# An encoder layer on one core: the product of memory values and output weight leaves the first stage and becomes filler work, per head, in the chain and mLSTM stages

## The chip, the cores and the metric

The kernel runs on one core of a Trainium2 chip. The metric is device time in microseconds. In a profile PE is TensorE (PEld its weight loads), DVE is VectorE, ACT is ScalarE, POOL is GpSimd and SP is SyncE, which issues nearly all DMAs; L115 is line 115 of the kernel.

## The reference, cut to what matters

One layer with a mixer (an input projection of the normalised x, four head groups that end in one output projection) and a cross-attention of 4 heads into 256 memory tokens. The change concerns the values of the cross-attention:

```
def memory_cross_attention(h, mem_n, wq, wkv, wo):
    q = split_heads(h @ wq, N_MEM_HEADS)
    k, v = jnp.split(mem_n @ wkv, 2, axis=-1)
    k, v = split_heads(k, N_MEM_HEADS), split_heads(v, N_MEM_HEADS)
    logits = jnp.einsum("bhtd,bhmd->bhtm", q, k).astype(jnp.float32) * (MEM_HEAD_DIM ** -0.5)
    p = jax.nn.softmax(logits, axis=-1)
    o = jnp.einsum("bhtm,bhmd->bhtd", p.astype(v.dtype), v)
    return merge_heads(o) @ wo
```

The memory is 256 x 1024, wkv 1024 x 2048, wo 1024 x 1024, x 1024 x 1024. Both kernels use that (p v) wo = p (v wo): for each head they form v wo, a matrix of 256 x 1024 from 256 x 256 and 256 x 1024, store it in DRAM as vwd, and multiply the probabilities with it at the very end. Only when and how v wo is formed changes.

## The kernel before, in words

Each large product is made of three (mm3, lines 137 to 139): operands are split into a high and a low part, and high x high, high x low and low x high are added in PSUM. Weights are split by wload (lines 111 to 127): a DMA brings 256 KB into a raw tile wr (128 x 512 values), ScalarE casts it to wh (line 122), and wl = raw - wh is formed by VectorE (line 124) while the extra pool wp0 is open, by GpSimd (line 126) afterwards. Pool wp1 has two raw tiles and four each of wh and wl; wp0, open in the first stage only, adds as many. Tiles of a kind are taken in turn, so a load waits until the raw tile two loads back has been read, and a cast until the wh tile four loads back has been used by its last product.

The stages on PE are these. **First stage**: eight column pieces of mem x wkv (loop over cp, 48 products of 256 columns each; pieces 0 to 3 are k, stored to kTd; 4 to 7 are v, split into tiles KV). Beside it x is normalised (xnorm, lines 238 to 246) and transposed (xhalf, lines 248 to 255, 16 transposes of 128 x 128 per call and four evacuations, a cast and a VectorE operation each). Then vwrow forms v wo from KV: per head 24 products of 512 columns, copied by ScalarE and stored to vwd; vwprep loads wo, four loads a head; two calls of xhalf stand between heads.

**Input projection and RWKV**: from here PE's order is written by hand. Projections are generators in the list fillers, and fill(n) draws n units from it in order of the list; a unit is one mm3 of 512 columns or two of 256. cproj and cprep prepare the recurrence, cgram makes its grams, and cinv inverts 32 x 32 blocks on VectorE in 31 steps. The inverse goes to DRAM and comes back turned (dTn, dTt), and tinv uses it on PE; fill(NI) with NI = 57 stands before that. Then cchain runs 16 steps, each with three fills of 2 units, and "while fillers: fill(1)" empties the list. The fillers at cgram are 128 units (DQ, DK, AV, AQ); 64 more (AK, CZ) join before the chain.

**mLSTM**: fillers bgemm, BZ, AZ (96 units); fill(G0), fill(G1), then eight steps, each with fill(GA), the products e v (L1059) and C q (L1066), fill(GB) before the products k v (L1095), fill(GC), and foxop, which loads rows of rT into tiles u for the next stage. Forgetting attention, the output projection and cross-attention follow and aren't touched; they use vwd last.

The order on other engines and on SP is a scheduler's, by program order and priority; wload runs at high priority. SP issues its DMAs in that order, so a DMA that waits for its tile holds back those behind it.

Of the kernel before, what the change touches and what calls it, by code (L numbers as in the profile page):

```python
# [8 lines left out]
F32 = mybir.dt.float32  # L9
F32R = mybir.dt.float32r  # L10
# [15 lines left out]
O_AQ, O_AK, O_AV, O_AG, O_AZ = 0, 256, 512, 768, 776  # L26
O_BX, O_BZ = 1032, 1288
# [9 lines left out]
def tile_trunk(ctx: ExitStack, tc: tile.TileContext, a, out, dbg=None):  # L37
# [30 lines left out]
    cur = {"wp0": None}  # L68
# [14 lines left out]
    def ps(tag, shape):  # L83
        return cur["ps"][tag](tag, shape)
# [51 lines left out]
    def mm3(o, lh, ll, rh, rl, st, sp, skip=False):  # L136
        T.matmul(o, lh, rh, start=st, stop=False, skip_group_check=skip)  # L137
        T.matmul(o, lh, rl, start=False, stop=False, skip_group_check=skip)  # L138
        T.matmul(o, ll, rh, start=False, stop=sp, skip_group_check=skip)  # L139
# [18 lines left out]
    def split_evac(hi, lo, p, scale=None):  # L158
        if scale is None:
            SC.copy(hi, p)  # L160
            V.tensor_tensor(lo, p, f32(hi), op=ALU.subtract)  # L161
        else:
            SC.activation(hi, p, AF.Copy, scale=scale)
            V.scalar_tensor_tensor(lo, p, scale, f32(hi), op0=ALU.mult, op1=ALU.subtract)
# [3 lines left out]
    dTt = dp.tile([128, 32, 32], F32, name="dTt")  # L168
    dTn = dp.tile([128, 32, 32], F32, name="dTn")
    vwd = dp.tile([1024, 1024], F32, name="vwd")  # L170
    zT = dp.tile([1024, 1024], F32, name="zT")
    rT = dp.tile([1024, 1024], F32, name="rT")
    x1d = dp.tile([1024, 1024], F32, name="x1d")
# [3 lines left out]
    dvd = dp.tile([1024, 256], F32, name="dvd")  # L177

    psum(mm=4, tr=4)
    m0 = Pool("m0", {"mT": 4, "KV": 4, "row": 2, "kv": 2})  # L180
    xp = Pool("xp", {"x": 2, "xn": 6})
    cur["wp0"] = Pool("wp0", {"wr": 2, "wh": 4, "wl": 4})


# [53 lines left out]
    def xnorm(i):  # L238
        x_t = xp("x", [128, 1024])
        SY.dma_start(x_t, a["x"][0, i * 128:(i + 1) * 128, :])  # L240
        xn = xp("xn", [128, 1024])
        r = base("tn", [128, 1])
        SC.activation(xn, x_t, AF.Square, accum_out=r)
        r = rstd_pow("tn", r, D, EPS)
        V.tensor_scalar(xn, x_t, r, None, op0=ALU.mult)
        xn_.append(xn)

    def xhalf(hf, k0, nk):

        for k in range(k0, k0 + nk):  # L250
            p = ps("tr", [128, 4, 128])
            for i in range(4):
                T.transpose(p[:, i, :], xn_[4 * hf + i][:, k * 128:(k + 1) * 128], ident)
            w = 2 * hf + k // 4
            split_evac(hTh[w][:, k % 4, :], hTl[w][:, k % 4, :], p.rearrange("p a b -> p (a b)"), pg[:, k:k + 1])

    Vh = [m0("KV", [128, 4, 256], F32R) for _ in range(2)]
    Vl = [m0("KV", [128, 4, 256], F32R) for _ in range(2)]
    xn_ = []
    for cp in range(8):  # L260
        p = ps("mm", [128, 2, 256])
        for k in range(8):
            if k % 2 == 0:
                wp = wk0[k // 2] if cp == 0 else wload(wv[:, cp, k:k + 2, :])
            wh, wl = (w_[:, k % 2, :] for w_ in wp)
            for c in range(2):
                cs = slice(c * 128, (c + 1) * 128)
                mm3(p[:, c, :], wh[:, cs], wl[:, cs], mTh[k // 4][:, k % 4, :], mTl[k // 4][:, k % 4, :],
                    k == 0 and c == 0, k == 7, True)
        if cp == 0:  # L270
            memnorm()
        t = m0("kv", [128, 2, 256])
        V.tensor_tensor(t, p, RS[:, cp // 4, None, :].to_broadcast([128, 2, 256]), op=ALU.mult)
        if cp < 4:
            SY.dma_start(kTd[cp * 256:(cp + 1) * 256, :].rearrange("(c p) m -> p c m", p=128), t)
        else:
            q, r = divmod(2 * cp - 8, 4)
            split_evac(Vh[q][:, r:r + 2, :], Vl[q][:, r:r + 2, :], t)
        xnorm(cp)
        if cp in (4, 5):  # L280
            xhalf(0, 4 * cp - 16, 4)


    incl = m0.one("incl", [128, 128])
# [35 lines left out]
    gcol = c2.one("gcol", [128, 4, 32])  # L320
    decb = c2.one("decb", [128, 2, 8])


    def vwprep(h):
        return [[wload(a["xattn_wo"][0, h * 256 + j * 128:h * 256 + (j + 1) * 128, q * 512:(q + 1) * 512]) for q in range(2)]
                for j in range(2)]

    def vwrow(h, wo_):
        for mt in range(2):
            vrow = m0("row", [128, 1024])  # L330
            for q in range(2):
                p = ps("mm", [128, 512])
                for j in range(2):
                    ct = 2 * h + j
                    ms = slice(mt * 128, (mt + 1) * 128)
                    mm3(p, Vh[ct // 4][:, ct % 4, ms], Vl[ct // 4][:, ct % 4, ms],
                        *wo_[j][q], j == 0, j == 1)
                SC.copy(vrow[:, q * 512:(q + 1) * 512], p)
            SY.dma_start(vwd[(2 * h + mt) * 128:(2 * h + mt + 1) * 128, :], vrow)

    w = vwprep(0)
    for h in range(4):
        nxt = vwprep(h + 1) if h < 3 else None
        vwrow(h, w)
        if h < 2:
            xhalf(1, 4 * h, 4)
        w = nxt
    w_in = a["w_in"][0]
    cur["wp0"].close()
    cur["wp0"] = None  # L350
# [99 lines left out]
    def ngemm_h(wd, c0, act, evac, nt=4):  # L450

        w = []
        for t0 in range(0, NT, nt):
            p = [ps("mm", [128, 2, 256]) for _ in range(nt // 2)]
            for k, wh, wl in (w or wpiece(wd, c0, 256, 2)):
                if t0 == 0 and nt < NT:
                    w = w + [(k, wh, wl)]
                for i in range(nt):
                    mm3(p[i // 2][:, i % 2, :], *act(t0 + i, k), wh, wl, k == 0 and i % 2 == 0, k == 7, True)
                    yield  # L460
            for i in range(nt):
                evac(t0 + i, p[i // 2][:, i % 2, :])

    def hact(i, k):
        return hslice(k, i * 128, 128)
# [184 lines left out]
            SC.copy(SV[c - 1][0:64, 1::2, :], p[0:64, :, 64:128])  # L650

    FA, FB, FC = 2, 2, 2
    NI = 57
    BN = {}

    def cbk(c):
# [289 lines left out]
    with tc.manual_schedule(engines={PE}):  # L946
        run(cproj(6, 1))
        run(cproj(2, 2))
        fillers += [cproj(0, 2), cproj(4, 2), vgemm(O_DV, 260, 8, dvd)]
        gs = [cnorm(hf, j) for hf in range(2) for j in range(2)]  # L950
        for g in gs:
            next(g)
            fill(6)
            run(g)
        fill(9)
        with tc.issue_after(act["cnorm"].ins), tc.issue_after(act["cproj"].ins):
            SC.activation(shifted[6][0:64, :], shifted[6][0:64, :], AF.Tanh)
            csplit(0)
        fill(5)
        gs = [cprep(hf, j) for hf in range(2) for j in range(2)]  # L960
        for n, g in enumerate(gs):
            with tc.issue_after(act["cnorm"].ins):
                next(g)
            if g is gs[-1]:
                act["ln"] = tc.keep_in_program_order(SC.preload_act_table_set("natural_log_exp_and_others"))
            fill(15)
            if n:
                run(gs[n - 1])
        fill(13)
        run(gs[-1])  # L970
        c1.close()
        fillers += [rgemm(O_DQ, 66, 0, 46, (7, 5, 5, 5)), rgemm(O_DK, 68, 256, 47, (6, 6, 5, 5)), vgemm(O_AV, 264, 0, avd), rgemm(O_AQ, 0, 512)]
        cc = Pool("cc", {"bq": 2, "n4": 4, "pr": 1, "t11": 1, "sv": 3, "ik": 2, "bn": 2, "w": 1, "uu": 1,
                         "bv": 1, "yc": 1, "ysb": 1})
        for _ in range(2):
            t = cc("ik", [128, 4, 64])
            for x in range(2):
                V.tensor_copy(t[PH[x], x::2, :], ident[PH[x], None, x * 64:(x + 1) * 64].to_broadcast([64, 2, 64]))
            IK.append(t)
        cprop(0)  # L980
        V.memset(SV[0][0:64, 0::2, :], 0.0)
        V.memset(SV[0][64:128, 1::2, :], 0.0)
        cgram(0, 2)
        cgram(1, 2)
        cinv()
        ti = [tinv(0), tinv(1)]
        next(ti[0])
        fill(NI)
        next(ti[0])
        fill(4)  # L990
        run(ti[0])
        fill(3)
        fillers += [rgemm(O_AK, 2, 768), zgemm(O_CZ, 2)]
        gr, ac = gaterows(), aconv()
        tc.cur_priority = 150000
        cprop(1)
        cbk(0)
        for c in range(16):
            cchain(c)
            if c < 3:  # L1000
                next(ti[1], None)
            if c >= 3:
                next(gr, None)
            if c >= 9:
                next(ac, None)
        run(ac)
        cstore()
        while fillers:
            fill(1)
# [144 lines left out]
            V.tensor_tensor(hi[r2], raw[r2], f32(hi[r2]), op=ALU.subtract)  # L1154
            qst[h] = hi

    fillers += [bgemm(), zgemm(O_BZ, 1), zgemm(O_AZ, 0)]
    G0, G1, GA, GB, GC = 14, 7, 2, 3, 4
    bp = [bpool(0), bpool(1)]
    with tc.manual_schedule(engines={PE}):  # L1160
        fill(G0)
# [422 lines left out]
```

## Time and profile before

| what | us |
|---|---|
| time, median of 3 runs | 952.8 (950.78 to 954.29) |
| time of the profiled execution | 948.88 |
| its span | 946.7 |
| memory projections, first products to the last | 8.6 to 61.9 |
| v wo products and x transposes | 61.9 to 88.1 |
| first product of tinv | 282.1 |
| chain, first step to last | 295.2 to 428.9 |
| list emptied, then fill(G0) | 428.9 to 449.8 |
| mLSTM steps, to the last k v or C q | 449.8 to 531.2 |

The span runs from the first to the last instruction; the other 2.2 us of the time lie around it. The granted clock is 0.985 on average. A matmul's own duration in the trace (0.28 us for 256 columns) is longer than the distance from one start to the next, since matmuls overlap; how many run in a stretch is what counts. Idle time of an engine is put down to what ended it.

### The profile page before, as it was taken

The page shows a single profiled execution, that of the slowest core. Times are in us where ns is not written, and L with a number is a line of the kernel's source. Part 1 is how long each engine was busy: PE and PEld are TensorE (multiplying, and loading weights), DVE is VectorE, ACT ScalarE, POOL GpSimd, SP SyncE. Part 2 cuts the span into 40 slices and gives each one's busy share as a digit, 9 for nine tenths or more (in the row PEclk, how much of TensorE's full clock was granted, in tenths as well). Part 3 has the DMA queues.
Part 4 walks back from the last instruction along what each step waited for, and adds up shares of the span by engine and source line. Part 5 has one row for each costly group of instructions (what it writes and reads, how often), then busy time and mean ns, then how long its engine had stood idle before and what let it go on. Part 6 is the DMA issues. An engine that isn't in the chain of part 4 may idle for free. (4 is left out here: it accounts for less than half of the span.)

```text
span 946.7 us, 16207 instructions
## 1 busy us (share of the span) xinstructions
PE 896.4 (95%) x6041; PEld 758.0 (80%) x6041; DVE 559.6 (59%) x1293; ACT 425.5 (45%) x981; POOL 205.5 (22%) x228
## 2 busy tenths in 40 slices
PE   6999999989978999989988999999999999999997
PEld 6998887877868877767766677788887888889997
DVE  7684047978672445664588566665675455554225
ACT  7686165330534435544444244534464443444221
POOL 1002222121310343543334732000000000121211
PEclk9999999989998999999999999999999999999999
DMA  8967211121233214135574677632246301143104
GB/s 285 296 220 237 79 45 46 34 84 35 90 112 81 83 29 125 40 123 132 139 174 127 201 244 223 177 116 90 90 136 211 100 23 46 34 173 110 43 1 178
DMA packets 94302, 113.85 MB, mean 120 GB/s; under 512 B 20944, under 2 KB 68624, under 8 KB 94224
## 3 DMA queue, kind: packets, MB, share of 16 engines
q1 hardware_dynamic: 94080, 112.71, 38.7%
q8 instruction: 48, 0.79, 0.4%
q14 instruction: 30, 0.25, 0.1%
q10 hardware_dynamic: 144, 0.11, 0.1%
HBM read 83.92 MB, written 28.87 MB: 119 GB/s over the span
## 5 line engine op out<-in xcount | busy, mean ns | idle before, releaser
L137 PE MATMUL mm<-h,wh 128*128 128x512 f32 x528 | 219.6, 416 | 1.4 <-DVE zu L766 1.1
L138 PE MATMUL mm<-l,wh 128*128 128x512 f32 x528 | 208.9, 396 | 0.0
L139 PE MATMUL mm<-h,wl 128*128 128x512 f32 x528 | 208.7, 395 | 0.0
L126 POOL TENSOR_TENSOR wl<-wr,wh 128x512 fp32r<-128x512 f32 (+2 forms) x74 | 100.9, 1365 | 420.8 <-ACT wh L122 382.8
L137 PEld LDWEIGHTS mm<-h,wh 128*128 128x128 f32 x528 | 100.0, 189 | 25.9 <-issue 1.8
L139 PEld LDWEIGHTS mm<-h,wl 128*128 128x128 f32 x528 | 100.0, 189 | 22.9
L122 ACT CAST wh<-wr 128x512 fp32r<-128x512 f32 (+2 forms) x122 | 74.6, 620 | 94.0 <-PE mm L138 46.8
L138 PEld LDWEIGHTS mm<-l,wh 128*128 128x128 f32 x528 | 100.4, 190 | 17.7 <-issue 0.8
L137 PE MATMUL mm<-wh,act 128*128 128x256 f32 x256 | 72.7, 284 | 0.0
L138 PE MATMUL mm<-wl,act 128*128 128x256 f32 x256 | 71.9, 281 | 0.0
L139 PE MATMUL mm<-wh,act 128*128 128x256 f32 x256 | 71.8, 281 | 0.0
L137 PE MATMUL mm<-h,act 128*128 128x512 f32 x128 | 53.6, 418 | 1.4 <-ACT jk L1325 0.9
L139 PE MATMUL mm<-h,act 128*128 128x512 f32 x128 | 50.4, 394 | 0.0
L138 PE MATMUL mm<-l,act 128*128 128x512 f32 x128 | 50.2, 392 | 0.0
L137 PEld LDWEIGHTS mm<-wh,act 128*128 128x128 f32 x256 | 48.3, 188 | 0.1
L138 PEld LDWEIGHTS mm<-wl,act 128*128 128x128 f32 x256 | 48.3, 188 | 0.0
L139 PEld LDWEIGHTS mm<-wh,act 128*128 128x128 f32 x256 | 48.1, 188 | 0.0
L137 PE MATMUL mm<-mT,wh 128*128 128x256 f32 x128 | 37.3, 291 | 8.6 <-ACT wh L122 8.6
L1514 DVE TENSOR_TENSOR o<-mm,gb 128x256 f32<-128x256 f32 x32 | 13.6, 424 | 43.8 <-ACT junk L1513 43.5
L137 PE MATMUL mm<-wh,h 128*128 128x260 f32 (+1 forms) x128 | 38.5, 301 | 1.0 <-DVE v L485 0.8
L139 PE MATMUL mm<-mT,wl 128*128 128x256 f32 x128 | 37.0, 289 | 0.6 <-DVE wl L124 0.5
L1460 ACT ACTIVATE e<-lgp,tf,r 128x256 f32<-128x256 f32 x32 | 18.0, 564 | 43.1 <-DVE tf L1457 43.1
(406 smaller groups left out, 1991.2 us busy)
## 6 DMA issues: line engine op xcount, KB each, us to landing
wr<-in_w_in_dram SPq DMA_DIRECT2D x50, 256.0 KB, 2.8
wr<-in_wkv_dram SPq DMA_DIRECT2D x32, 256.0 KB, 4.3
x<-in_x_dram SPq DMA_DIRECT2D x16, 512.0 KB, 5.4
x<-x1d SPq DMA_DIRECT2D x15, 512.0 KB, 5.4
wr<-in_xattn_wo_dram SPq DMA_DIRECT2D x16, 256.0 KB, 3.2
vwd<-row SPq DMA_DIRECT2D x8, 512.0 KB, 4.2
rT<-zu SPq DMA_DIRECT2D x16, 256.0 KB, 2.4
zT<-zu SPq DMA_DIRECT2D x16, 256.0 KB, 3.1
```

The costliest lines, as they stand in the source:

```text
L122: SC.copy(hi, raw)
L126: G.tensor_tensor(lo, raw, f32(hi), op=ALU.subtract)
L137: T.matmul(o, lh, rh, start=st, stop=False, skip_group_check=skip)
L138: T.matmul(o, lh, rl, start=False, stop=False, skip_group_check=skip)
L139: T.matmul(o, ll, rh, start=False, stop=sp, skip_group_check=skip)
L1460: SC.activation(e, p, AF.Exp, bias=nb, scale=r2[:, i:i + 1], accum_out=dn)
L1514: V.tensor_tensor(o3[i][:, gs], p, xog[:, gs], op=ALU.mult)
```

## The change

The products v wo leave the first stage. The pieces 4 to 7 are stored to DRAM (vTd), as the k pieces are, instead of being split into KV. All x loads and norms are placed in pieces 0 to 5 (ten xn tiles instead of six), and the four calls of xhalf follow pieces 4 to 7. vwgemm(h) is a new generator of 8 units: for each quarter q of the columns of wo it loads a 256 x 256 piece of wo, and for every second quarter the head's v again, 6 loads of 256 KB a head; 12 products of 256 columns, a copy and a store of 256 KB to vwd in each quarter. Heads 0 and 1 join the fillers behind CZ before the chain, heads 2 and 3 between BZ and AZ. NI goes from 57 to 67, GB from 3 to 5, and the fill ahead of the second half of the last cprep from 13 to 18. Lines behind the first stage have numbers lower by 9 in the changed kernel.

```diff
+    vTd = dp.tile([1024, 256], F32, name="vTd")
...
-    m0 = Pool("m0", {"mT": 4, "KV": 4, "row": 2, "kv": 2})
-    xp = Pool("xp", {"x": 2, "xn": 6})
+    m0 = Pool("m0", {"mT": 4, "kv": 2})
+    xp = Pool("xp", {"x": 2, "xn": 10})
...
-        if cp < 4:
-            SY.dma_start(kTd[cp * 256:(cp + 1) * 256, :].rearrange("(c p) m -> p c m", p=128), t)
-        else:
-            q, r = divmod(2 * cp - 8, 4)
-            split_evac(Vh[q][:, r:r + 2, :], Vl[q][:, r:r + 2, :], t)
-        xnorm(cp)
-        if cp in (4, 5):
-            xhalf(0, 4 * cp - 16, 4)
+        SY.dma_start((vTd if cp > 3 else kTd)[cp % 4 * 256:(cp % 4 + 1) * 256, :].rearrange("(c p) m -> p c m", p=128), t)
+        if cp < 6:
+            xnorm(cp)
+        if cp in (3, 4):
+            xnorm(cp + 3)
+        if cp > 3:
+            xhalf(cp // 6, 4 * (cp % 2), 4)
...
-    w = vwprep(0)
-    for h in range(4):
-        nxt = vwprep(h + 1) if h < 3 else None
-        vwrow(h, w)
-        if h < 2:
-            xhalf(1, 4 * h, 4)
-        w = nxt
...
+    def vwgemm(h):
+
+        hs = slice(h * 256, (h + 1) * 256)
+        for q in range(4):
+            qs = slice(q * 256, (q + 1) * 256)
+            if q % 2 == 0:
+                vh, vl = wload(vTd[hs].rearrange("(j p) m -> p j m", p=128))
+            wh, wl = wload(a["xattn_wo"][0, hs, qs].rearrange("(j p) c -> p j c", p=128))
+            p = ps("mm", [128, 2, 256])
+            for mt in range(2):
+                ms = slice(mt * 128, (mt + 1) * 128)
+                for j in range(2):
+                    mm3(p[:, mt, :], vh[:, j, ms], vl[:, j, ms], wh[:, j, :], wl[:, j, :], mt == 0 and j == 0, j == 1, True)
+                    yield 0.5
+            z = cur["stg"]("zu", [128, 2, 256])
+            SC.copy(z, p)
+            SY.dma_start(vwd[hs, qs].rearrange("(t p) c -> p t c", p=128), z)
...
-    NI = 57
+    NI = 67
...
-        fill(13)
+        fill(18)
...
-        fillers += [rgemm(O_AK, 2, 768), zgemm(O_CZ, 2)]
+        fillers += [rgemm(O_AK, 2, 768), zgemm(O_CZ, 2), vwgemm(0), vwgemm(1)]
...
-    fillers += [bgemm(), zgemm(O_BZ, 1), zgemm(O_AZ, 0)]
-    G0, G1, GA, GB, GC = 14, 7, 2, 3, 4
+    fillers += [bgemm(), zgemm(O_BZ, 1), vwgemm(2), vwgemm(3), zgemm(O_AZ, 0)]
+    G0, G1, GA, GB, GC = 14, 7, 2, 5, 4
```

On PE, behind the chain: before, the last product of CZ is followed by the first of bgemm (h and l are x turned and split, wh and wl the weight).

```order
L137 MATMUL mm_4445<-h_161,wh_4698 128x512
L138 MATMUL mm_4445<-l_165,wh_4698 128x512
L139 MATMUL mm_4445<-h_161,wl_4699 128x512
L137 MATMUL mm_4791<-h_158,wh_4797 128x512
L138 MATMUL mm_4791<-l_162,wh_4797 128x512
L139 MATMUL mm_4791<-h_158,wl_4798 128x512
```

In the changed kernel the same place reads so (wh_4505 is the head's v, wh_4511 a piece of wo):

```order
L137 MATMUL mm_4083<-h_162,wh_4409 128x512
L138 MATMUL mm_4083<-l_166,wh_4409 128x512
L139 MATMUL mm_4083<-h_162,wl_4410 128x512
L137 MATMUL mm_4515<-wh_4511,wh_4505 128x256
L138 MATMUL mm_4515<-wl_4512,wh_4505 128x256
L139 MATMUL mm_4515<-wh_4511,wl_4506 128x256
```

96 such products of heads 0 and 1 now stand there in one piece. CZ's last 18 products stand between the chain's last step and them, where 48 stood before.

On SP, the loads for that place: before, those of CZ and bgemm (wr), among stores of yc and rT.

```order
L115 DMA wr_4666<-in_w_in_dram 128x2x256
L738 DMA yu<-yc_4132 128x256
L115 DMA wr_4696<-in_w_in_dram 128x2x256
L115 DMA wr_4795<-in_w_in_dram 128x2x256
L738 DMA yu<-yc_4296 128x256
L798 DMA rT<-zu_4430 128x512
```

Now loads of v and wo take turns with the stores of their results.

```order
L115 DMA wr_4581<-in_xattn_wo_dram 128x2x256
L762 DMA zT<-zu_4491 128x512
L115 DMA wr_4603<-vTd 128x2x256
L762 DMA zT<-zu_4497 128x512
L453 DMA vwd<-zu_4528 128x2x256
L115 DMA wr_4609<-in_xattn_wo_dram 128x2x256
L453 DMA vwd<-zu_4550 128x2x256
L115 DMA wr_4631<-in_xattn_wo_dram 128x2x256
```

A store to vwd stands ahead of the load three tiles on, and waits for the products that it stores.

On SP in the mLSTM steps: before, the loads of u for foxop and of e and v for the next step stand between two weight loads.

```order
L115 DMA wr_5689<-in_w_in_dram 128x2x256
L1084 DMA yu<-hh_5141 128x256
L1146 DMA u_5530<-rT 64x1024
L1043 DMA e_5437<-cd 128x512
L1146 DMA u_5530<-rT 64x1024
L1041 DMA v_4786<-avd 128x4x64
L1146 DMA u_5634<-rT 64x1024 x2
L115 DMA wr_5839<-in_w_in_dram 128x2x256
```

Now they stand between the loads of one head's v and wo:

```order
L115 DMA wr_5401<-vTd 128x2x256
L1032 DMA v_4738<-avd 128x4x64
L1137 DMA u_5665<-rT 64x1024 x2
L1137 DMA u_5781<-rT 64x1024
L115 DMA wr_5407<-in_xattn_wo_dram 128x2x256
L1075 DMA yu<-hh_5106 128x256
L1034 DMA e_5521<-cd 128x512
L1137 DMA u_5781<-rT 64x1024
```

The load of wo, wr_5407, comes behind u_5665 and half of u_5781, which are foxop's rows of steps 5 and 6.

More of the change, by code (lines that the diff above doesn't have):

```diff
@@ L245, in xnorm @@
         V.tensor_scalar(xn, x_t, r, None, op0=ALU.mult)
-        xn_.append(xn)
+        xn_[i] = xn
     def xhalf(hf, k0, nk):
@@ L255, in xhalf @@
             split_evac(hTh[w][:, k % 4, :], hTl[w][:, k % 4, :], p.rearrange("p a b -> p (a b)"), pg[:, k:k + 1])
-    Vh = [m0("KV", [128, 4, 256], F32R) for _ in range(2)]
-    Vl = [m0("KV", [128, 4, 256], F32R) for _ in range(2)]
-    xn_ = []
+    xn_ = {}
     for cp in range(8):
@@ L321, in tile_trunk @@
     decb = c2.one("decb", [128, 2, 8])
[L324 to L339, printed above, removed]
-    w = vwprep(0)
-    for h in range(4):
-        nxt = vwprep(h + 1) if h < 3 else None
-        vwrow(h, w)
-        if h < 2:
-            xhalf(1, 4 * h, 4)
-        w = nxt
     w_in = a["w_in"][0]
```

## The prediction

> **What bounds the kernel now.** I read the page first, then busy times cut at the stages, then the waits at the places that the change touches.
>
> ```profile
> span 946.7 us, 16207 instructions
> PE 896.4 (95%) x6041; PEld 758.0 (80%) x6041; DVE 559.6 (59%) x1293; ACT 425.5 (45%) x981; POOL 205.5 (22%) x228
> ```
>
> TensorE (PE) is busy 95% of the span, so moving products from one stage to another pays only what idle it fills, and costs what idle it makes. The stages (columns: busy us and instructions of each engine, then granted clock, DMA share, GB/s):
>
> ```profile
> core 0: us, PE busy (x) PEld busy (x) DVE busy (x) ACT busy (x) POOL busy (x), PEclk, DMA share, GB/s
> 0.00:61.90 61.90, 52.19 (x418) 51.41 (x419) 47.24 (x96) 44.40 (x79) 8.36 (x22) 1.00 0.83 272
> 61.90:88.10 26.20, 26.08 (x130) 21.40 (x129) 15.78 (x26) 19.00 (x36) 2.54 (x2) 1.00 0.71 224
> 201.90:275.80 73.90, 69.35 (x407) 56.56 (x406) 58.41 (x121) 23.39 (x46) 14.91 (x13) 0.93 0.27 74
> 275.80:282.10 6.30, 0.27 (x3) 0.06 (x2) 3.42 (x9) 1.11 (x2) 1.03 (x2) 0.78 0.56 188
> 282.10:295.20 13.10, 13.07 (x174) 12.86 (x175) 3.51 (x7) 4.26 (x11) 0.00 (x0) 0.72 0.31 71
> 295.20:428.90 133.70, 126.17 (x1210) 100.76 (x1208) 70.82 (x173) 64.48 (x198) 49.35 (x55) 0.99 0.27 79
> 428.90:449.80 20.90, 20.90 (x94) 16.79 (x92) 8.15 (x16) 9.29 (x21) 8.79 (x10) 1.00 0.57 150
> 449.80:531.20 81.40, 75.33 (x471) 59.03 (x470) 61.35 (x140) 33.40 (x73) 34.09 (x31) 1.00 0.58 159
> 531.20:552.00 20.80, 17.53 (x64) 12.05 (x63) 11.42 (x22) 5.67 (x10) 17.40 (x22) 0.92 0.53 169
> ```
>
> In order: memory projections and x transposes; the product stage; the grams and the inverse; the hole before tinv; tinv; the chain; its tail, in which PE empties the fillers; the mLSTM loop; what follows it. PE is covered nearly everywhere. The one large hole is 275.8 to 282.1, and behind it the clock is 0.72. The mLSTM loop has small holes.
>
> **Part A, the first stage.** 96 products of 512 columns and their 16 loads leave it; the 64 x transposes stay, 32 of them moved from between the products to after projections 6 and 7. What these things cost on PE:
>
> ```profile
> core 0: us, PE busy (x), PEclk, DMA share, GB/s
> 50.50:61.90 11.40, 11.40 (x99) 1.00 0.63 202
> 67.50:69.10 1.60, 1.60 (x16) 1.00 0.95 367
> ```
>
> About 96 products of 256 columns take 11.4 us, 0.12 each; 16 transposes take 1.6. So the stage ends at 61.9 + 2 x 1.6 = 65.1 instead of 88.1: -23.0. VectorE keeps 4 splits (686 ns) and 4 evacuations (744) per projection:
>
> ```profile
> 40.50:61.90 21.40, 20.85 (x178) 20.62 (x178) 19.71 (x31) 17.41 (x31) 1.91 (x4) 1.00 0.74 241
> L124 DVE TENSOR_TENSOR wl<-wr,wh 128x512 fp32r<-128x512 f32 x48 | 31.4, 686 | 7.1 <-ACT wh L122 7.0
> L164 DVE SCALAR_TENSOR_TENSOR l<-tr,cst,h 128x512 fp32r<-128x512 f32 x16 | 11.4, 744 | 0.7 <-ACT h L163 0.7
> ```
>
> Its work from 40.5 on becomes 19.7 - 4 x 0.69 + 8 x 0.74 = 22.9 us in 24.6: close behind PE. I allow 3 us for its lag and for the first w_in tile, which now has no product stage to land under: **A = -20** (-23 if all is hidden, -13 if VectorE sets the pace with its waits). x loads keep their places between the weight loads on SP's queue, and the vTd stores take the place of the larger vwd ones.
>
> **Part C, the hole before tinv.** It waits for the inverse to come back from DRAM, not for PE:
>
> ```profile
> 282.13 2.07 PE L625 MATMUL sm<-t,bq 32*32 32x32 f32 x39 [6.06 <-DMA t<-dTn]
> ```
>
> NI 57 to 67 puts 10 units there, 60 products of 264 columns and 8 of onesr: 68 x 0.12 = 8.2 us, so tinv starts at 284.1, 2 us late. But its 13.1 us ran at clock 0.72; at 1.00 they are 13.1 x 0.72 = 9.4, a gain of 3.7. With a microsecond for two norms that no longer sit in the first chain steps, **C = -3** (from -6 to +2). VectorE's inverse has no new instruction ahead of it. fill(13) to fill(18) changes nothing: the fills ahead ask for 24 + 9 + 5 + 60 = 98 units and the three fillers hold 96.
>
> **Part D, the tail of the chain.** A chain step spends six units as before, so what is new falls behind the chain. 112 units less 96 left 16 there; now 102 + 16 less 96 leave 22: six of CZ, then heads 0 and 1 whole. By the 20.90 us that 94 product records took, a 512-column product is 0.222 us, a unit 0.67. The tail and the 14 units of fill(G0) were 20.9. Now 6 x 0.67 + 96 x 0.12 + 14 x 0.67 = 24.9 if every weight is ready: +4.0.
>
> They will not be. A unit of the old fillers uses an eighth of a load; two heads need 12 loads for 11.5 us of products. What a load costs here:
>
> ```profile
> L122 ACT CAST wh<-wr x17: 603/618/622, 396.8 to 532.7; 128x512 fp32r<-128x512 f32 x17
> L126 POOL TENSOR_TENSOR wl<-wr,wh x17: 1266/1285/1803, 397.5 to 537.9; 128x512 fp32r<-128x512 f32 x17
> DMA to landing us min/median/max: 2.5/2.8/5.8
> ```
>
> And the buffers are two: the next load is issued when GpSimd's subtraction has read the raw tile.
>
> ```profile
> 233.33 1.29 POOL L126 TENSOR_TENSOR wl<-wr,wh 128x512 fp32r<-128x512 f32 x1 [9.47 <-ACT wh L122]
> 234.65 0.39 SPq L115 DMA_DIRECT2D wr<-in_w_in_dram  x1
> ```
>
> One buffer turns round in 2.8 + 0.62 + 1.29 + some 0.3 of hand-over = 5.0 us, so a load comes every 2.5 us while PE could use one every 11.5 / 12 = 0.96. Three tiles are ready when head 0 starts (four wh tiles, one still held by CZ). Stepped through, PE waits 2.1 before the third quarter (its cast needs the tile that the second quarter frees), 0.7, 3.6 before head 1, 1.4, 3.6, 0.7, and 1.4 before bgemm's first tile: 13.5 us. **D = +4.0 + 13.5 = +17.5** (+4 without waits, +22 with landings of 3.8).
>
> **Part E, the mLSTM loop.** Heads 2 and 3 add 11.5 us of products. GB 5 spends two more units where PE waits for VectorE's ks, seven times. PE's waits from 449 to 552:
>
> ```profile
> PE ml L1095 <- DVE ks L1091: 3.4, 3, 1.5
> PE ml L1066 <- DVE e L1052: 2.7, 3, 1.7
> PE ml L1134 <- DVE u L1135: 2.2, 1, 2.2
> PE mm L137 <- DVE zu L766: 1.1, 1, 1.1
> ```
>
> 9.4 us in all; a later PE lets VectorE catch up, and I take 7 of them as filled. The same 12 loads at 2.5 us now run in steps 3 to 5, with small products between: stepped through, 2.1 + 3.0 + 2.3 + 2.9 = 10.3 us of waits. **E = 11.5 - 7 + 10.3 = +15** (+2 without waits, +26 if nothing is filled and landings are 3.8).
>
> GpSimd's 12 more subtractions can also hold VectorE up. The row: beside one, an operation of 0.42 us takes 1.43.
>
> ```profile
> 263.99 0.42 DVE L603 TENSOR_TENSOR n<-n,pr 128x252 f32<-128x252 f32 x1
> 264.09 1.51 POOL L126 TENSOR_TENSOR wl<-wr,wh 128x528 fp32r<-128x528 f32 x1 [4.58 <-ACT wh L122]
> 264.45 1.43 DVE L601 TENSOR_TENSOR pr<-n,n 128x247 f32<-128x247 f32 x1
> ```
>
> In the loop that is at most 12 x 1.0 us of VectorE, which has 20 us idle of 81 there; I count none on the path. The Trainium skill ("GPSIMD Engine Reference", 8. Key points) names shared SBUF interfaces for VectorE instructions with two SBUF inputs as the cause.
>
> **The sum.** -20 - 3 + 17.5 + 15 = +9.5. The profiled execution took 948.9 (span 946.7 and 2.2 around it): 958.4. It lies 3.9 under the median 952.8; shifted alike, 962 for a median.
>
> **The rivals.**
> Loads keep up (faster): if reloads overlap better than two buffers seem to allow, D is +4, E 11.5 - 7 = +4.5, the sum -14.5: 938. For it: the projections of stage 1 ran with almost no waits. Against: four raw buffers there, and VectorE doing the subtraction. It decides where the waits of D and E together fall under 9.5 us: then the change is faster by over 0.5%. Chance 0.20.
> Waits half hidden: 12 us of 24, the sum -2.3: 950.5. For it: some of E's waits lie under VectorE's own. 0.18.
> The first stage is bound by VectorE: A -13, the sum +16.5: 969. For it: 22.9 of 24.6 us. Against: these same operations ran at 19.7 of 21.4 with 0.6 us of PE idle. 0.11.
> SP's queue holds loads back: in the loop, loads of u, which wait for buffers that VectorE frees, stand ahead of the vw loads; E is +26, the sum +20.5: 973. 0.10.
> The forecast as it stands: 0.41, its own range 954 to 970.
>
> The clock could add to it: after the 6.3 us hole the row says 0.78, then 0.72. The Trainium skill ("TensorE: Matmul & The Clock Gate", Part 1: The HAM clock gate) drops to half rate after about one idle window of 3.4 us. By that rule the two waits of 3.6 us would each cost half a 3.4 us window, 1.7 us: an estimate of +3.4. The trace agrees for the long hole; for 3.6 us no row here decides it.
>
> **How the numbers follow.** A measurement of this kernel tells about 0.5%, 4.8 us, from no change. Slower: 0.41 + 0.11 + 0.10 = 0.62; same 0.18; faster 0.20. The range of 8 in 10 reaches to the rival of loads that keep up and to that of the held queue, with the bounds of the landings beyond: 938 to 978.
>
> **What would show it.** Right: cproj's first product near 68 us; no hole ahead of tinv and clock 1.00 there; in the chain's tail and in loop steps 3 to 5, PE waits of 2 to 4 us for wh or wl at products with 256 columns, with casts about 2.5 us apart. Wrong: these products running back to back at 0.12 us, a first stage ending later than 72, or vw loads issued late though a raw buffer was free.

## The result and the profile after

The changed kernel takes 977.7 us (median, 976.2 to 981.3), the kernel before 952.7 beside it: a ratio of 1.027 (95% interval 1.023 to 1.030). It is slower by 25 us, where 9 were forecast. The profiled executions lie 28.3 apart, 975.0 against 946.7 us of span. The page of the changed kernel:

```profile
span 975.0 us, 16464 instructions
PE 913.6 (94%) x6137; PEld 775.4 (80%) x6137; DVE 551.5 (57%) x1273; ACT 429.6 (44%) x985; POOL 235.7 (24%) x252
```

Of the 28.3 us, 17.2 are busy time of PE, although its products come to the same number of columns. Most of this is the half clock: products of 256 columns start 0.21 us apart at clock 0.50 (behind 436.97) and 0.12 at 1.00 (behind 433.26), and PE spends 49.8 us of its busy time at half clock, where it spent 22.4; half of the difference is 13.7. Busy times of the changed kernel cut at its own stages: first stage; product stage of the projections; grams, inverse and the fill ahead of tinv; tinv; chain; tail; loop; what follows it.

```profile
core 0: us, PE busy (x) PEld busy (x) DVE busy (x) ACT busy (x) POOL busy (x), PEclk, DMA share, GB/s
0.00:70.49 70.49, 56.90 (x450) 54.69 (x451) 49.52 (x101) 48.42 (x84) 13.43 (x31) 1.00 0.79 251
70.49:187.50 117.01, 114.56 (x584) 95.86 (x584) 64.92 (x112) 47.90 (x83) 24.25 (x20) 0.97 0.17 44
187.50:276.69 89.19, 79.40 (x476) 66.24 (x475) 66.34 (x139) 30.24 (x65) 15.84 (x15) 0.92 0.32 90
276.69:287.07 10.38, 10.38 (x179) 10.15 (x179) 2.12 (x3) 3.66 (x7) 2.24 (x2) 1.00 0.35 96
287.07:408.98 121.91, 121.49 (x1168) 96.32 (x1166) 66.65 (x169) 61.14 (x189) 49.26 (x56) 1.00 0.26 78
408.98:452.04 43.06, 32.74 (x159) 27.40 (x157) 8.72 (x14) 19.00 (x36) 21.40 (x19) 0.80 0.66 193
452.04:556.51 104.47, 93.10 (x561) 76.44 (x560) 66.38 (x140) 45.21 (x94) 49.13 (x45) 0.92 0.61 173
556.51:574.69 18.18, 16.64 (x64) 11.63 (x63) 11.50 (x19) 5.44 (x10) 17.65 (x21) 1.00 0.56 182
```

The clock is low where the new products stand (0.80 and 0.92), and tinv and the chain run at full clock. With the same borders in the other profiled executions (each is the start of the first product of the next stage; the border after the first is the last small product ahead of the grams, 201.91 in the kernel before) five kernels give the table on which the rest leans. The two in the middle columns are explained below: "no products" leaves the moved products out (and has the old GB 3), "few loads" makes them with 2 loads a head in place of 6. GB differs too: it is 3 in the first three columns and 5 in the last two, and the profiled execution of "few loads" lies 4.2 us above its median.

| stage, us | before | before, NI 67 | change, no products | change, few loads | change |
|---|---|---|---|---|---|
| to the last small product (A) | 201.9 | 203.6 | 187.9 | 190.0 | 187.5 |
| from there to the chain's end (C) | 226.9 | 221.1 | 221.6 | 221.7 | 221.5 |
| tail (D) | 20.9 | 14.1 | 14.1 | 26.0 | 43.1 |
| loop and the stretch behind it (E) | 101.5 | 107.2 | 108.7 | 114.8 | 122.7 |
| the rest | 395.5 | 395.0 | 397.2 | 403.5 | 400.3 |
| span | 946.7 | 941.0 | 929.4 | 956.0 | 975.0 |
| median of all runs | 952.7 | 943.5 | 928.7 | 953.6 | 977.7 |

Measured against forecast: A -14.4 (-20), C -5.5 (-3), D +22.1 (+17.5), E +21.2 (+15), the rest +4.9 (0); together +28.3 (+9.5). PE's waits in the tail, then in the loop and behind it, of the changed kernel (us in total, times, longest):

```profile
PE mm L137 <- ACT wh L122: 4.9, 3, 2.6
PE mm L138 <- POOL wl L126: 4.7, 5, 2.0
PE mm L139 <- POOL wl L126: 0.6, 1, 0.6
```

```profile
PE mm L138 <- POOL wl L126: 6.3, 3, 4.2
PE ml L1079 <- ACT nu L1052: 2.4, 2, 1.4
PE ml L1125 <- DVE u L1126: 1.4, 1, 1.4
PE ml L1057 <- DVE e L1043: 1.4, 1, 1.4
PE mm L137 <- ACT wh L122: 1.1, 1, 1.1
```

Both stretches wait for wh and wl, as forecast. One raw buffer's turn in the tail, by start and length; first SP, with the issue of its load and of the next load into it:

```profile
424.03 0.38 SPq L115 DMA_DIRECT2D wr<-in_xattn_wo_dram  x1
...
429.28 0.36 SPq L115 DMA_DIRECT2D wr<-vTd  x1
```

Then the cast on ScalarE:

```profile
427.29 0.62 ACT L122 CAST wh<-wr 128x512 fp32r<-128x512 f32 x1
```

And the subtraction on GpSimd, which frees the buffer:

```profile
427.99 1.26 POOL L126 TENSOR_TENSOR wl<-wr,wh 128x512 fp32r<-128x512 f32 x1 [2.54 <-ACT wh L122]
```

It takes 5.25 us (429.28 - 424.03); the forecast had 5.0. It is one of the shorter turns. The eight loads issued in the tail from 408.88 to 434.58 took 9.46, 7.16, 7.13, 5.25, 6.16, 5.30, 4.93 and 5.08 us from their issue to that of the next load into the same buffer, 6.3 on average. They landed after 2.7 to 5.2 us, 3.6 on average, where the forecast had 2.8.

### The profile page after: what moved, and what is told of

It is laid out like the page before. It is cut to its first block, busy times and chain, and to the rows that moved or that the text cites. A ratio compares the mean times of both kernels' runs of the same rounds, so it can differ in the third digit from the quotient of the medians.

```text
span 975.0 us, 16464 instructions
## 1 busy us (share of the span) xinstructions
PE 913.6 (94%) x6137; PEld 775.4 (80%) x6137; DVE 551.5 (57%) x1273; ACT 429.6 (44%) x985; POOL 235.7 (24%) x252
## 5 line engine op out<-in xcount | busy, mean ns | idle before, releaser
L126 POOL TENSOR_TENSOR wl<-wr,wh 128x512 fp32r<-128x512 f32 (+2 forms) x98 | 133.2, 1361 | 412.9 <-ACT wh L122 377.8
L122 ACT CAST wh<-wr 128x512 fp32r<-128x512 f32 (+2 forms) x130 | 79.6, 617 | 119.5 <-PE mm L138 43.8
L139 PEld LDWEIGHTS mm<-h,wl 128*128 128x128 f32 x528 | 100.5, 190 | 24.1 <-POOL wl L126 1.1
L138 PEld LDWEIGHTS mm<-l,wh 128*128 128x128 f32 x528 | 100.7, 191 | 17.5 <-issue 0.5
L138 PE MATMUL mm<-wl,h 128*128 128x260 f32 (+1 forms) x128 | 37.7, 295 | 0.0
L139 PE MATMUL mm<-wh,l 128*128 128x260 f32 (+1 forms) x128 | 37.6, 294 | 0.0
```

Of the source, the lines that this page charges most:

```text
L122: SC.copy(hi, raw)
L126: G.tensor_tensor(lo, raw, f32(hi), op=ALU.subtract)
```

## The experiments

Times are medians; a ratio is to the kernel before, run on the same chip.

### NI alone, from both sides

The changed kernel with the old NI (ni57), and the kernel before with the new one (before_ni67):

```
-    NI = 67          in the changed kernel
+    NI = 57
-    NI = 57          in the kernel before
+    NI = 67
```

> The changed kernel with NI back at 57. Measured in the changed kernel: tinv's first product comes 89.2 us after the last evacuation of cprep's small sums, 80.2 before the change, and the chain from its first product takes 121.9 us, 133.2 before. Theory: the ten units added at NI lead PE into a copy that waits, over a store of rT, for the loads of the inverse on SP's queue; without them tinv comes at about 80 us again, with its hole of 6 us. If the shorter chain is also owed to those ten units (they were taken out of its way), the chain takes about 132 again and the time stays within 3 us of the changed kernel's 977.7. Rival: the shorter chain has another cause; then it stays at 122 and the time falls by 6 to 9 us, to 969 to 972.

> The kernel before with NI = 67 and nothing else. Theory (the chain's gain is owed to NI): tinv 6 to 9 us later, chain 8 to 11 shorter, time within 3 us of 952.7 or somewhat below. Rival (the chain's gain is owed to something else in the change): tinv later by 6 to 9 us, chain 133, time 958 to 962.

Measured: 982.9 (ratio 1.034, 1.031 to 1.037) and 943.5 (0.992, 0.989 to 0.995). NI 67 is worth 5 us in the one and 8 in the other. It does not close the hole ahead of tinv. In the changed kernel PE still waits there, one step earlier:

```profile
PE mm L137 <- ACT gates L744: 5.1, 1, 5.1
```

ScalarE waits for a staging tile whose store stands on SP's queue behind the loads of the inverse:

```profile
264.39 0.93 SPq L606 DMA_DIRECT2D t<-dTn  x2
...
267.95 0.49 SPq L608 DMA_DIRECT2D n<-dTt  x1
268.48 0.96 SPq L789 DMA_DIRECT2D rT<-zu  x2
```

The gain is tinv at full clock and a chain nearly without waits: its 133.2 us become 121.7. In the changed kernel its waits come to 0.4 us; before they were:

```profile
PE cw L674 <- ACT ysb L706: 3.5, 3, 1.9
PE sm L646 <- ACT bn L665: 1.8, 1, 1.8
PE cs L688 <- DVE w L676: 1.3, 2, 0.7
PE cs L694 <- DVE uu L690: 0.7, 1, 0.7
```

With NI 57 in the changed kernel they are back (4.8 us). That they go with NI is shown; by which of the shifted instructions was not tried.

### The loads: few_loads

The first load of v and the first wo tile serve all four quarters of a head (left out: the other loads, with their casts and subtractions, so vwd holds other numbers; the code is cut at the dots):

```
-            if q % 2 == 0:
+            if q == 0:
                 vh, vl = wload(vTd[hs]...)
-            wh, wl = wload(a["xattn_wo"][0, hs, qs]...)
+            if q == 0:
+                wh, wl = wload(a["xattn_wo"][0, hs, qs]...)
```

> The changed kernel, in which a head loads v and one piece of wo once and uses them for all four quarters: 2 loads a head instead of 6, the products, copies and stores are all there (vwd then holds the wrong products, the time of what reads it is the same). Theory of the supply (two raw tiles, 2.5 us a load): PE's waits for wh and wl at the products of 256 columns, 16 us in the tail and 9 in the mLSTM steps by start distances, nearly vanish; time 950 to 957. Rival (the products fill no idle time there, and the copies and stores queue): the time falls by less than 8 us, to 970 or more.

Measured: 953.6 (ratio 1.002, 0.999 to 1.005; single executions from 948.5 to 959.2), 24 us under the changed kernel. The 16 loads cost 24 us. The tail is then PE's products alone:

```profile
411.67:437.67 26.00, 25.60 (x159) 22.50 (x157) 6.07 (x13) 11.11 (x20) 11.27 (x11) 1.00 0.70 209
```

26.0 us at full clock; the forecast's figure for a tail with every weight ready was 24.9.

### Deeper buffers, a shorter turn: deep_tail and vec_split

deep_tail closes the chain's pool when the chain ends and gives its space to two more raw tiles and four more of wh and wl while the list is emptied (not shown: a flag that keeps the subtraction on GpSimd, and the old place of cc.close()):

```
+        cc.close()
+        cur["wp0"] = Pool("wp0b", {'wr': 2, 'wh': 4, 'wl': 4})
         while fillers:
             fill(1)
+        cur["wp0"].close()
```

> The changed kernel; the pool of the chain is closed before the list of fillers is emptied, and a second weight pool of 2 raw, 4 wh and 4 wl tiles is open while it is emptied, so that 4 raw tiles serve heads 0 and 1; nothing else. Theory of the supply: twice the raw tiles bring a load every 1.3 us or so (GpSimd's subtraction sets it), the 28 us of the 96 products fall to 16 to 18, time 966 to 969. Rival (GpSimd, ScalarE's order or the queue sets the pace, not the raw tiles): the products still take 25 us or more, time 974 to 978.

Measured: 974.7 (1.025, 1.021 to 1.029). The space comes free only when the chain has ended, and the first new loads are waited for at once; afterwards GpSimd's subtractions run back to back, five in 6.21 us:

```profile
PE mm L137 <- ACT wh L122: 7.6, 1, 7.6
PE mm L138 <- POOL wl L126: 1.9, 2, 1.1
```

```profile
422.83 6.21 POOL L126 TENSOR_TENSOR wl<-wr,wh 128x512 fp32r<-128x512 f32 x5 [1.88 <-ACT wh L122]
```

So four raw tiles about double the pace (1.24 us a load in this burst, where the turn of 5.25 gives 2.6 with two), and the late start takes most of it back: the tail is 37.3 us in place of 43.1.

vec_split forms wl of the moved weights on VectorE (0.69 us in place of 1.29), one link of the turn cut short (not shown: the argument vec, which is true for these loads alone):

```
-            if cur["wp0"] is not None:
+            if cur["wp0"] is not None or vec:
                 V.tensor_tensor(lo, raw, f32(hi), op=ALU.subtract)
```

> The changed kernel with the subtraction of the vw weights on VectorE (0.69 us) in place of GpSimd (1.29 us); TensorE's order is the same, nothing is left out. Theory that the turn-round of two raw buffers (landing, cast, subtraction, hand-over: 5.0 us by the prediction) sets the pace: 0.6 us less for each round, 0.3 for each of 24 loads: 7 us less, 968 to 973. Rival, that the landing of the loads or SP's queue sets it: 976 to 980. Rival, that VectorE's own steps in the loop are delayed by the twelve subtractions there: 979 to 985.

Measured: 975.9 (1.026, 1.022 to 1.029); the tail stays 43.05 us. In the tail most waits only change their name, from wl to wh:

```profile
PE mm L137 <- ACT wh L122: 7.2, 3, 4.5
PE mm L138 <- DVE wl L124: 0.3, 1, 0.3
```

0.6 us off the subtraction brought nothing that the medians show, so the sum of links with one fixed landing is not the whole of the pace: in the tail of this run too the loads land after 2.7 to 5.3 us. The loop and the stretch behind it are 119.1 us in the profiled execution, 3.6 less; the medians, with spreads that overlap, are 1.8 apart. How much each link takes was not separated.

### The half clock: keep_busy and keep_busy2

In the changed kernel a slice of 3.4 us with PE 36% busy, whose idle time is two waits of 1.2 and 1.0 us, is followed by a slice at half clock:

```profile
433.18:436.60 3.42, 1.24 (x9) 0.83 (x8) 0.00 (x0) 1.12 (x3) 2.57 (x2) 1.00 0.75 222
436.60:440.01 3.41, 3.24 (x13) 2.94 (x14) 0.00 (x0) 1.20 (x2) 1.28 (x1) 0.50 0.86 226
```

Slices at half clock held 11.6 us of busy PE in the tail and 15.9 in the loop. Half of it, 13.7 us, is more than the 10.8 by which D and E lie over the forecast. Both runs give PE products on a constant to do ahead of each quarter, which need no weight:

```
             p = ps("mm", [128, 2, 256])
+            for _ in range((24, 8)[q % 2] // (1 + h // 2)):      keep_busy2: (10, 4)
+                T.matmul(p[:, 0, 0:128], ident, ident, start=True, stop=True, ...)
```

> The changed kernel (977.7 us), where each quarter of a vw product is preceded by idle-time products of 128 columns on a constant (24 and 8 in turn for heads 0 and 1, 12 and 4 for heads 2 and 3: 96 products, about 0.11 us each, 64 x 0.11 = 7.0 us in the chain's tail for each 64, 3.5 in the loop); their result is overwritten by the real products. They need no weight, so TensorE works while it waits for one. Theory that the half clock is the missing term: in the changed kernel the slices at granted clock 0.5 in the tail (419.5 to 433.2, 436.6 to 440.0) and in the loop (508.3 to 511.7, 521.9 to 535.6) held 11.6 and 15.7 us of busy TensorE, which at full clock would have been 5.8 and 7.9 us shorter; with the extra products most of these windows go, and the time falls to 966 to 973 although TensorE has more to do. Rival, that only the supply of weights counts: the loads come as late as before, the extra products lie in the waits or lengthen them: 977 to 985, and the granted clock may be 1.00 there all the same.

> The run keep_busy again with fewer extra products, since each of them turned out to be two records of 0.11 us, so that 28 us of them stood in the chain's tail where 16.5 us were idle. Now 10 and 4 a quarter for heads 0 and 1 (56 x 0.22 = 12.3 us in the tail), 5 and 2 for heads 2 and 3 (6.2 us in the loop). Theory that the half clock costs in these two stretches what its busy time says (5.8 and 7.9 us): 966 to 972. Rival, that the weights set the pace there and slower products only use up what would be idle: 974 to 981 though the clock is 1.00.

Measured: 993.3 (1.046, 1.043 to 1.048) for the first, with too many of them, and 977.3 (1.028, 1.026 to 1.029) for the second. The second's tail and loop:

```profile
410.54:457.69 47.15, 41.14 (x271) 36.89 (x268) 10.32 (x16) 21.14 (x42) 22.80 (x20) 0.96 0.65 188
457.69:561.69 104.00, 95.00 (x617) 78.35 (x616) 64.54 (x138) 42.50 (x88) 50.47 (x47) 0.97 0.61 171
```

The clock rises from 0.80 to 0.96 and from 0.92 to 0.97, and the time is the same. The loop is 104.0 us, where it was 104.5. The tail is 4 us longer, with 12.3 us of extra products in it; PE still waits 5.9 us there, and two of its loads land only after 5.3 and 6.4 us. My theory, that the half clock was the missing term here, fell: no time came back. For the tail the trace of the changed kernel shows why. From 418.34 to 434.58 each load is issued 0.03 us after the subtraction that frees its buffer, and is cast 0.02 to 0.50 us after it lands, so that no load waits for PE, and slower products use up time that would be idle. For the loop the run does not separate what the clock brought from what the 6.2 us of extra products cost.

### A hole that PE could have filled: before_ni67_hole

The kernel before with NI 67; the filler products that follow are put on the list one step earlier, so that eight units lie in the hole ahead of the last small product:

```
-        fill(13)
+        fill(8)
+        fillers += [rgemm(O_DQ, ...), rgemm(O_DK, ...), vgemm(O_AV, ...), rgemm(O_AQ, ...)]
+        fill(8)
         run(gs[-1])
         c1.close()
-        fillers += [rgemm(O_DQ, ...), rgemm(O_DK, ...), vgemm(O_AV, ...), rgemm(O_AQ, ...)]
```

> The kernel before with NI 67 (943.5 us), where the filler products that follow the first four projections are made available one step earlier, so that 8 units (24 products of 512 columns, 5.3 us) can be spent in the hole ahead of the last small product (TensorE idle 4.03 us at 203.6, then granted clock 0.5 for 6.8 us). Nothing is added or left out. Theory that a hole costs its length and half of the busy time in the slices at half clock behind it: 4.0 + 4.1 us at most, less the 1.3 us by which 5.3 us of products are longer than the hole: 935 to 939. Rival, that a hole costs only its idle time: 940 to 942. Rival, that the products are only moved and a hole comes back ahead of tinv: 942 to 946.

Measured: 934.1 (0.983, 0.981 to 0.985), 9.4 us under NI 67 alone, for a hole of 4.0 us. The hole and what stands behind it without the edit, then the same places with it:

```profile
203.57:207.61 4.04, 0.26 (x4) 0.20 (x3) 4.01 (x6) 0.68 (x2) 1.71 (x1) 0.90 0.26 65
207.61:213.60 5.99, 5.64 (x29) 4.82 (x30) 3.72 (x14) 0.26 (x1) 0.00 (x0) 0.50 0.51 154
```

```profile
204.28:208.30 4.02, 4.02 (x20) 3.32 (x20) 3.99 (x6) 0.61 (x2) 1.36 (x1) 1.00 0.24 65
208.30:214.30 6.00, 6.00 (x43) 4.70 (x41) 4.41 (x14) 0.88 (x2) 1.27 (x1) 1.00 0.62 192
```

3.8 us idle (4.04 less 0.26) and 5.64 busy at 0.50 (2.8 lost) are 6.6 of the 9.4. So the hole cost more than its idle time; that the 2.8 us are the half clock's is worked out and not shown by a run of its own, but here PE had its next products ready. By stages, tinv starts 0.5 us earlier with eight units already done (292.0 against 292.5), the way from there to the loop is 5.6 us shorter (140.6 against 146.2), and the loop with the stretch behind it 2.6 (104.6 against 107.2). This is the fastest kernel of the study that leaves nothing out; it beats both, and does not contain the change of place.

### The first stage by itself: no_vw, no_vw_gb3, no_vw_clean

All three leave out the moved products and store zeros. The first two store them where the products' results were stored; the second has GB 3 in place of 5. The third stores them from one tile in the stage behind the first, with GB 3:

```
-        fillers += [rgemm(O_AK, 2, 768), zgemm(O_CZ, 2), vwgemm(0), vwgemm(1)]
+        fillers += [rgemm(O_AK, 2, 768), zgemm(O_CZ, 2)]
-    fillers += [bgemm(), zgemm(O_BZ, 1), vwgemm(2), vwgemm(3), zgemm(O_AZ, 0)]
-    G0, G1, GA, GB, GC = 14, 7, 2, 5, 4
+    fillers += [bgemm(), zgemm(O_BZ, 1), zgemm(O_AZ, 0)]
+    G0, G1, GA, GB, GC = 14, 7, 2, 3, 4
```

> The changed kernel without the pending products: the two chain units and the two mLSTM units only store zeros, no weights are loaded for them and no products made (left out: the product of memory values and output weight). What is left of the change is the shorter first stage, NI 67 and GB 5. Theory that the first stage gains the 14.4 us seen at the last small product before the holes (201.9 against 187.5) and keeps them to the end: the kernel before with NI 67 alone (943.5 us) less 14.4: 929 (925 to 933). The prediction's own size for the first stage, 20 us: 923. Rival, that an earlier first stage is handed back by later waits (GB 5 and a shorter tail): 936 to 944.

> The changed kernel without the pending products (left out: the product of memory values and output weight; zeros are stored) and with GB 3, as the kernel before has it. In the run with GB 5 (939.9 us) the loop's fillers were used up early and its last steps ran uncovered, so that it did not show the first stage's gain by itself. Theory that the 14.4 us gained by the last small product before the holes last to the end: 943.5 less 14.4: 929 (926 to 933). The prediction's own size, 20 us: 923. Rival, that what follows the first stage takes part of it back whatever GB is: 936 to 942.

> The changed kernel with GB 3 and without the pending products (left out: the product of memory values and output weight). Unlike the run no_vw_gb3 it stores the zeros from one tile in the stage behind the first, where the DMA queue has little to do, and not in 16 stores at the start of the mLSTM loop, where they stood ahead of the load of the gate rows (TensorE waited 6.0 us for it there). Theory that the first stage's 14.4 us last to the end once nothing stands in the loop for them: 943.5 less 14.4: 929 (926 to 934). Rival, that the loop and what follows it are bound by other engines, so that an earlier start is given back whatever TensorE has to do: 938 to 944.

Measured: 939.9 (0.989, 0.987 to 0.992), 943.8 (0.993, 0.991 to 0.994) and 928.7 (0.977, 0.974 to 0.979). The first two were spoilt by their own stores; in the first, with GB 5, PE also stands 7.2 us behind the loop. In the second the stores stand on SP's queue ahead of the load of the gate rows, for which VectorE, and PE behind it, stand near the loop's start:

```profile
PE ml L1033 <- DVE e L1035: 6.0, 1, 6.0
```

The clean run gives the answer: the first stage's gain is kept, 943.5 - 928.7 = 14.8 us by the medians (the profiled spans, 941.0 and 929.4, lie 11.6 apart). From there the two halves of the products' price follow from the medians: 928.7 to 953.6, 25 us for the products with a third of their loads, in which the change of GB from 3 to 5 is contained; 953.6 to 977.7, 24 us for the other loads.

### GB: after_gb3

```
-    G0, G1, GA, GB, GC = 14, 7, 2, 5, 4
+    G0, G1, GA, GB, GC = 14, 7, 2, 3, 4
```

> The changed kernel with GB 3 in place of 5, as in the kernel before: two units fewer at seven places of the mLSTM loop, where TensorE waits for VectorE's ks; the 14 units (9.4 us) are spent behind the loop. If GB 5 fills 7 us of waits, as the prediction had it, the waits come back and the time is 981 to 986. If the loop's waits are set by the weights and by VectorE's row of steps whatever lies between, it is 974 to 980, no measurable change. If GB 5 itself delays the loop: 968 to 974.

Measured: 974.1 (969.2 to 978.3; ratio 1.025, 1.020 to 1.029), 3.6 us less than with GB 5, with overlapping spreads: no gain from GB 5, and perhaps a loss. The loop with the stretch behind it takes as long (122.4 and 122.7 us); the rest is 396.5 against 400.3. The wait behind the loop, in the changed kernel and with GB 3:

```profile
PE tr L1281 <- DVE zt L1222: 3.7, 1, 3.7
```

```profile
PE tr L1281 <- DVE zt L1222: 1.1, 1, 1.1
```

### The end of the first stage: act_order

Two casts of ScalarE are put behind the eight x splits; all other orders stay (not shown: the branch that leaves every other cast where it was).

```
+            if 34 < wcount["wr"] < 37:
+                with tc.issue_after(cur["xs"].ins):
+                    SC.copy(hi, raw)
```

> The changed kernel with two casts of ScalarE moved behind the eight x splits at the end of the first stage (casts of the third and fourth w_in tile); every other engine's order is the same, nothing is left out. In the changed kernel ScalarE stood 3.5 us at 58.3 on the landing of that tile with the splits queued behind it, and TensorE waited 4.1 us for the splits. Theory that this place in ScalarE's queue, and not VectorE's amount of work, holds the first stage up: the first product of the next stage starts at 66 to 68.5 in place of 70.5, and the slice at half clock behind it goes (1.7 us). If that is kept to the end: 972 to 975. Rival, that VectorE sets the pace there: 70 to 71, 976 to 979. Rival, that the weights moved back come too late for the next stage: 977 to 981.

Measured: 979.7 (1.029, 1.027 to 1.031), no gain; the next stage's first product at 70.35, as with the change (70.49). ScalarE no longer stands on the landing, and then it waits 4.52 us for the transposes themselves:

```profile
66.85 2.42 ACT L167 ACTIVATE h<-tr,cst 128x512 fp32r<-128x512 f32 x4 [4.52 <-PE tr L258]
```

The theory of ScalarE's queue fell. PE's waits at the stage's end, in the changed kernel, and VectorE's last work there:

```profile
PE mm L137 <- DVE l L164: 2.6, 1, 2.6
PE tr L254 <- DVE l L164: 1.5, 2, 1.2
```

```profile
67.12 0.68 DVE L272 TENSOR_TENSOR kv<-mm,RS 128x512 f32<-128x512 f32 x1
67.71 2.72 DVE L164 SCALAR_TENSOR_TENSOR l<-tr,cst,h 128x512 fp32r<-128x512 f32 x4
```

The splits of the last transposes end at 70.4, and the next stage needs them. It is not the amount of VectorE's work: from 40.5 to 70.49 it is busy 22.7 of 30.0 us, and in act_order it stands idle right ahead of its last operations, until the last projection is done:

```profile
66.42 0.69 DVE L276 TENSOR_TENSOR kv<-mm,RS 128x512 f32<-128x512 f32 x1 [3.06 <-PE mm L143]
```

What the two runs have in common is that the last transposes, their casts and their splits follow one another at the end, with no product of PE beside them. That this order is the cause is read from the rows; no run with another was made.

## Why the prediction was wrong, step by step

The direction was right, and so was its main mechanism: PE waits for wh and wl at products of 256 columns, and with a third of the loads most of these waits go. The forecast's waits for loads were 13.5 and 10.3, 23.8 in all; the other loads cost 24.1 by the medians of few_loads and the changed kernel (16 of the 24 loads). That the two agree so well is luck in part: the waits are 17.1 in the tail and 7.9 in the loop, one more and one less than forecast. What failed:

**"A later PE lets VectorE catch up, and I take 7 of them as filled"** (part E). This step failed most, and not by the 7 itself. It took the loop of the kernel before, with its waits of 9.4 us, as the place into which the products go. By the time they come it is another loop. The loop with the stretch behind it, in the kernel before, without the products, and with few loads:

```profile
449.79:551.28 101.49, 92.16 (x527) 70.41 (x527) 72.46 (x159) 39.08 (x83) 51.50 (x52) 0.98 0.57 161
423.58:532.27 108.69, 96.65 (x527) 73.44 (x527) 73.21 (x161) 41.35 (x91) 50.32 (x51) 0.94 0.56 155
437.67:552.50 114.83, 107.66 (x623) 86.66 (x623) 71.48 (x161) 48.26 (x104) 55.59 (x56) 0.94 0.62 174
```

Before any new product stands in it, E is 7.2 us longer: the same 527 products keep PE busy for 96.65 us and not 92.16, at clock 0.94 and not 0.98, and 12.0 us are idle where 9.3 were. The products of heads 2 and 3 then fill 4.9 of these 12.0 (7.2 stay idle) and lengthen E by 6.1, where 11.5 - 7 = 4.5 were forecast; the other loads add 7.9 for 10.3. 7.2 + 6.1 + 7.9 make E's +21.2.

**What stands in E before any new product.** Of the 7.2, 5.7 come with NI 67 alone (kernel before) and 1.5 without the products in the first stage. The 7 us that NI takes out of the tail (20.9 to 14.1) were booked as a gain in D, and as nothing in E, which gives most of them back: its waits are for VectorE, and PE now comes to them earlier. What share of it is the half clock and what the waits was not separated.

**The rest.** It was put at nothing and grows by 4.9. With GB 3 the changed kernel's rest is 396.5, 1.0 over the kernel before, and without the products 397.2. So most of it seems to go with GB 5 and not with the products, as far as one profiled execution of each shows.

**A = -20.** The stage gave 14.4. It ended at 70.5 and not at 68.1 (65.1 and the 3 us allowed), because the last transposes' splits, which had lain under the product stage, now lie bare, as far as the rows show: 2.6 and 1.5 us of waits. The next 3.2 us are lost up to the last small product, where the changed kernel's row shows clock 0.97 and the same stretch before had 1.00. The rival with VectorE as the bound was near in size with -13, and named the engine that PE waits for, but not the reason: VectorE has time to spare there.

**D = +17.5.** It came to +22.1. With few loads it is +5.1 (+4.0 forecast), so the waits are 17.1 where 13.5 were stepped out. The mis-sized term is the turn, 6.3 us on average for 5.0. Its landings took 3.6 for 2.8, near the 3.8 for which the forecast's own bound was +22. The first turn after the chain took 9.46, from 408.88 to 418.34: its cast came 2.9 us after its landing, and its subtraction stood behind that of another tile, which had waited for the chain's last norm on GpSimd:

```profile
414.21 0.74 POOL L720 TENSOR_TENSOR yc<-yc,bv 128x256 f32<-128x256 f32 x1
414.91 3.40 POOL L126 TENSOR_TENSOR wl<-wr,wh 128x512 fp32r<-128x512 f32 x2
```

**C = -3.** It came to -5.5, but not as told: tinv starts at 276.69 and not at 269.7 (the forecast's 284.1 less the 14.4 of A), 7 us later, of which 5.1 are the wait behind the staging tile; and the chain gave 11.3 back. Two misses of opposite sign.

**The clock.** The Trainium skill ("TensorE: Matmul & The Clock Gate", Part 1: The HAM clock gate) gives about one idle window of 3.4 us for the drop, from a free-running window. The runs agree with the free-running window: in the changed kernel the half-clock stretches of tail and loop begin at 419.5, 436.6, 508.3 and 521.9, whole multiples of 3.41 us apart. They differ on the idle: a slice 36% busy was enough. The estimate of +3.4 was not borne out as a price either: keep_busy2 raised the clock and gained nothing, and 2.8 us are worked out behind one hole that PE could have used.

## What to carry to other kernels

Before work is moved under a wait, ask who ends the wait, and whether the place will still be the same when the work gets there: here the loop was 7.2 us longer before any moved product stood in it, and with a third of their loads the moved products cost 25 us by the medians, about their full length. Count the loads that moved work brings per microsecond of its own products, against the turn of the buffers at the place where it will stand: here 16 of 24 loads cost 24 us, as much as the 23 us of products that they served. Check what the old place hid, too: the evacuations that had lain under the products were bare once these were gone, and a stage that loses 23 us of products gave 14.8.

## What was not expected of the hardware

TensorE's clock fell to 0.50 after a slice of 3.4 us in which it was 36% busy, with no wait over 1.2 us. The busy share alone does not decide it: in the changed kernel a slice 69% busy (160.12 to 163.53) was followed by one at 0.50, in the kernel before one as busy (412.4 to 415.8) by one at 1.00. Half-clock slices cost 2.8 us by their busy time where products were ready (behind the hole at 203.6), and nothing that a run shows in the tail, where no load waited for PE: a clock of 0.96 in place of 0.80 there left the time at 977.3 against 977.7. Filling one hole of 4.0 us brought 9.4 us.
